# A two-block network on one core: the scheduler orders instructions on its timeline model

## The chip, the core and the metric

The kernel runs on one core of a Trainium2 chip, in one launch. The metric is the device time of that core in microseconds, the median of three runs. The engines are TensorE (PE: matmuls; PEld: its weight loads), VectorE (DVE), ScalarE (ACT), GpSimd (POOL) and SyncE (SP), which issues nearly all DMAs. Each engine works through its own list of instructions strictly in order, and semaphores make it wait for others.

## What is computed

The input is 256 tokens of width 1024, a context of 256 tokens, a condition vector and the weights of two blocks. The first block has four layers, the second has two:

```python
def first_block(x, p, ...):                     # DEPTH = 4
    for i in range(DEPTH):
        kind, j = i % N_MIXERS, i // N_MIXERS   # conv, ssm, rwkv, conv
        if kind == 0:
            y = short_conv_mixer(x, conv_w_in[j], conv_k[j], conv_w_out[j])
        elif kind == 1:
            y = s5_mixer(x, ...)
        else:
            y = rwkv7_mixer(x, ...)
        r = DN_ALPHA * x + y
        r = r + (p[i] @ ple_proj[i]) * jax.nn.sigmoid(r @ ple_gate[i])
        x = layer_norm(r, ln_g[i], ln_b[i])
    return x

def swiglu(h, w1, w3, w2):
    return (jax.nn.silu(h @ w1) * (h @ w3)) @ w2
```

Each layer of the second block is a half ffn (swiglu with 2816 hidden), a mixer and another half ffn, each behind an RMS norm that is shifted and scaled by values worked out from the condition (nine such vectors per layer and stream, called ada). Layer 0's mixer is attention of two kinds over tokens and context (mixer_ab), layer 1's is a chunked recurrence and a neighbourhood attention (mixer_cd). The context goes through ffns and the same attention of its own.

The parts that matter below are the rwkv mixer's end and the first conv:

```python
    mu_o = out.mean(-1, keepdims=True)
    var_o = jnp.square(out - mu_o).mean(-1, keepdims=True)
    out = ((out - mu_o) * lax.rsqrt(var_o + RWKV_GN_EPS)).reshape(bsz, seqlen, D_INNER)
    out = out * lnx_g.astype(f32) + lnx_b.astype(f32)
    ...
    return (out * jax.nn.silu(z)) @ w_out
```

## The kernel before

Activations lie transposed in SBUF, features on the 128 partitions in eight chunks, 256 tokens in the free direction. Every large product is done in three passes on values split in a high and a low part. `Net.get` (L590 to L607) brings in a weight tile of 128x1024 values: SP issues the DMA of 512 KB into `w` (L600), ScalarE copies the high part to `whi` (L601), VectorE subtracts it for the low part `wlo` (L602). `w` has four buffers, and `whi` and `wlo` four pairs. An output tile of 128x256 then takes 24 matmuls into a PSUM bank, eight chunks by three passes (`ps_mm`; three banks). Other banks are `ps_st` for sums over features, `ps_ca` and `ps_cb` for small products.

The program is written as Python generators, one for each chain of work (tokens, context, the heads of a mixer, preparation work on the side). `Net.weave` and `Net.par` pick which goes on, by a hand-made model of costs, and so lay down the program's order. Nothing of that is the engines' order yet. The kernel is recorded in a tile context (L1968), whose scheduler then goes through the program with the program's order as the priority: whenever an engine is free it takes the first instruction, in program order, that is ready by then. What "by then" means depends on a run of the program that the scheduler keeps beside it.

Three pieces of the program are spoken of later. In the first conv (`conv`, L720) the weights `in_conv_in` come as 32 tiles; while they stream, `ssm_prep` (L822) works on tables of the next layer on VectorE and ScalarE (tiles `ssm_s`, with DMAs `in_ssm_bc` at L891), and `load_context` (L1922) and `ada` (L1370) load `ctx` and `cond`. In `rwkv` (L1065), `heads` (L1178) runs for eight pairs of heads, up to three at a time on three sets of scratch (`rw_a0`, `rw_b0` to `rw_b2`). Each ends with four chunks of a state recurrence through `ps_cb` and `sv`, a norm over the head (`rsqrt`, L1336), and writes `r`. Behind the last of them the operand `mix` of the product for z takes the scratch slots of `rw_a1` and `rw_b1`, and `linear("rwkv_z", ...)` goes on with it. Beside all this the context's ffn runs (`ps_mm <- h1_hi, h1_lo`), which shares no data with the token stream. `rsqrt` (L679) is Ln, Exp and a square on ScalarE and two VectorE passes.

Where ScalarE's next function is not in the table that is loaded, an ACT_TABLE_LOAD stands before it; these are put in after the order is fixed.

## Time and profile before

| what | before |
|---|---|
| median of 3 runs | 2886.37 us (2886.14 to 2888.42) |
| profiled execution | 2890.76 us, of it 2889.0 us span from the first to the last instruction |
| TensorE busy | 2749.4 us (95% of the span) |
| VectorE busy | 2134.0 us (74%) |
| ScalarE busy | 1606.4 us (56%) |
| mean granted TensorE clock | 0.977 |
| DMA | 467.53 MB, engines busy 50% of the span |

The profiled execution is one execution of its own, with the profiler on; its time lies 4.4 us above the median of the others. An engine's busy share is a mean over very different stages.

### The profile page before, as it was taken

Reading aid. Unit: us, or ns where it says so; the run is one execution under the profiler, and the core shown is the slowest. Engines: PE = TensorE matmul, PEld = TensorE weight load, DVE = VectorE, ACT = ScalarE, POOL = GpSimd, SP = SyncE. Lnnn points to the kernel's source line nnn. Section 1 sums busy time; section 2 is a strip of 40 time slices with the busy share of each in tenths; the row PEclk is TensorE's granted clock in tenths of the full one; section 3 lists DMA queues with packets and bytes.
Section 4 is the critical chain, followed back from the end, with each engine's and each line's share of the span. In section 5 each row is a group of like instructions: output and inputs, shape, how many; then the busy total and the mean of one; then the engine's idle time right before and its main releaser. Section 6 shows DMA issues by size and latency. Waiting matters only on the chain.

```text
span 2889.0 us, 58552 instructions
## 1 busy us (share of the span) xinstructions
PE 2749.4 (95%) x23798; PEld 2604.6 (90%) x23798; DVE 2134.0 (74%) x3953; ACT 1606.4 (56%) x2976; POOL 14.8 (1%) x41
## 2 busy tenths in 40 slices
PE   8978799899999998999999999999999999999999
PEld 8967799778998998998999978999999999996999
DVE  8877777666688788899789887777855556676655
ACT  5455555766555465877666766445422234466443
POOL 0000000000000000000000000000000000000000
PEclk9989799999999999999999999999999999999999
DMA  7743355201586665666576644666543433222554
GB/s 270 238 165 110 108 167 175 82 17 40 163 269 226 220 197 167 209 215 203 182 226 195 199 130 155 203 225 194 180 142 125 139 117 103 89 82 65 161 182 139
DMA packets 132751, 467.53 MB, mean 162 GB/s; under 512 B 14720, under 2 KB 19072, under 8 KB 131840
## 3 DMA queue, kind: packets, MB, share of 16 engines
q1 hardware_dynamic: 132480, 463.78, 50.0%
q8 instruction: 187, 3.06, 0.4%
q14 instruction: 84, 0.69, 0.1%
HBM read 462.67 MB, written 1.05 MB: 161 GB/s over the span
## 4 chain that ended last, share of the span: by engine, by line
PE 72%; DVE 12%; DMA 7%; ACT 6%; issue 3%; SPq 0%; ACTq 0%; DVEq 0%
PE ps_mm L433 62%; PE ps_ca L433 5%; DMA w<-in_ada_dram 5%; DVE wlo L602 3%; PE ps_cb L433 2%; DVE junk L1379 2%; PE ps_st L433 2%; DVE ssm_m L403 2%; ACT whi L601 2%; DVE tc L403 1%; PE ps_cb L437 1%; ACT rw_b L403 1%; ACT L403 1%; ACT tc L403 1%; DMA w<-in_ab_in_dram 1%
## 5 line engine op out<-in xcount | busy, mean ns | idle before, releaser
L601 ACT ACTIVATE whi<-w 128x1024 fp32r<-128x1024 f32 (+1 forms) x687 | 715.9, 1043 | 740.2 <-PE ps_mm L433 488.1
L602 DVE TENSOR_TENSOR wlo<-w,whi 128x1024 fp32r<-128x1024 f32 (+1 forms) x687 | 825.6, 1203 | 239.2 <-ACT whi L601 236.8
L433 PE MATMUL ps_mm<-h_hi,whi 128*128 128x256 f32 x3024 | 873.1, 290 | 17.1 <-ACT h_hi L403 12.4
L433 PE MATMUL ps_mm<-h_hi,wlo 128*128 128x256 f32 x3024 | 859.5, 285 | 9.5 <-DVE wlo L602 9.5
L433 PE MATMUL ps_mm<-h_lo,whi 128*128 128x256 f32 x3024 | 856.5, 284 | 0.6 <-DVE h_lo L403 0.5
L433 PEld LDWEIGHTS ps_mm<-h_hi,whi 128*128 128x128 f32 x3024 | 573.6, 190 | 25.8 <-ACT h_hi L403 15.1
L433 PEld LDWEIGHTS ps_mm<-h_hi,wlo 128*128 128x128 f32 x3024 | 573.3, 190 | 12.2 <-DVE wlo L602 11.5
L433 PEld LDWEIGHTS ps_mm<-h_lo,whi 128*128 128x128 f32 x3024 | 577.5, 191 | 5.2 <-DVE h_lo L403 1.9
L1379 DVE SCALAR_TENSOR_TENSOR junk<-w,cond 128x1024 bf16<-128x1024 f32 x288 | 351.7, 1221 | 145.0 <-DMA w<-in_ada_dram 144.1
L433 PE MATMUL ps_mm<-d_hi,whi 128*128 128x256 f32 x1232 | 355.7, 289 | 4.1 <-DVE ctx L403 3.0
L433 PE MATMUL ps_mm<-d_hi,wlo 128*128 128x256 f32 x1232 | 350.4, 285 | 1.5 <-DVE wlo L602 1.5
L433 PE MATMUL ps_mm<-d_lo,whi 128*128 128x256 f32 x1232 | 349.2, 283 | 0.4 <-DVE d_lo L403 0.4
L433 PEld LDWEIGHTS ps_mm<-d_hi,whi 128*128 128x128 f32 x1232 | 232.3, 189 | 8.7 <-issue 5.7
L433 PEld LDWEIGHTS ps_mm<-d_lo,whi 128*128 128x128 f32 x1232 | 234.0, 190 | 3.4 <-issue 1.2
L433 PEld LDWEIGHTS ps_mm<-d_hi,wlo 128*128 128x128 f32 x1232 | 232.1, 189 | 2.8 <-DVE wlo L602 2.0
L403 DVE TENSOR_TENSOR td<-td,ps_mm 128x256 f32<-128x256 f32 x154 | 64.4, 418 | 70.0 <-PE ps_mm L433 68.9
L403 ACT ACTIVATE d_hi<-td 128x256 fp32r<-128x256 f32 x154 | 63.0, 409 | 89.5 <-DVE td L403 88.7
L403 ACT ACT_TABLE_LOAD x78 | 100.1, 1283 | 2.1 <-PEq L1964 0.7
L433 PE MATMUL ps_mm<-x_hi,whi 128*128 128x256 f32 x256 | 73.5, 287 | 12.0 <-ACT whi L601 12.0
L403 ACT ACTIVATE tc<-tc 128x256 f32<-128x256 f32 x182 | 75.1, 413 | 5.6 <-DVE tc L403 2.6
L433 PE MATMUL ps_mm<-xs_hi,whi 128*128 128x256 f32 x256 | 73.4, 288 | 4.8 <-ACT xs_hi L403 4.4
L403 ACT ACTIVATE td<-ps_mm 128x256 f32<-128x256 f32 x154 | 57.4, 374 | 32.9 <-PE ps_mm L433 32.3
(467 smaller groups left out, 5270.5 us busy)
## 6 DMA issues: line engine op xcount, KB each, us to landing
w<-in_ffn_in_dram SPq DMA_DIRECT2D x268, 512.0 KB, 4.2
w<-in_ada_dram SPq DMA_DIRECT2D x168, 512.0 KB, 4.3
w<-in_ffn_out_dram SPq DMA_DIRECT2D x96, 512.0 KB, 4.1
w<-in_conv_in_dram SPq DMA_DIRECT2D x64, 512.0 KB, 4.7
w<-in_ffn_out_dram SPq DMA_DIRECT2D x48, 384.0 KB, 3.1
w<-in_ab_in_dram SPq DMA_DIRECT2D x34, 512.0 KB, 4.4
w<-in_ple_gate_dram SPq DMA_DIRECT2D x32, 512.0 KB, 4.5
w<-in_conv_out_dram SPq DMA_DIRECT2D x16, 512.0 KB, 5.2
```

Of the source, the lines that this page charges most:

```text
L403: return f(**kw)
L433: self.t.matmul(out, lhsT=lhsT, rhs=rhs, start=start, stop=stop)
L437: self.t.transpose(out, in_, ident)
L601: nc.scalar.activation(out=hi[:, :n], in_=w[:, :n], func=AF.Copy)
L602: nc.vector.tensor_tensor(out=lo[:, :n], in0=w[:, :n], in1=hi[:, :n].bitcast(F32), op=ALU.subtract)
L1379: nc.vector.scalar_tensor_tensor(out=self.junk, in0=w, scalar=1.0, in1=cb[:, s], op0=ALU.mult, op1=ALU.mult, accum_out=m[:, t, s:s + 1])
```

## The change

One argument of the tile context: the scheduler keeps its timeline model beside it, instead of executing the program, to find out what is ready when.

```diff
@@ -1965,7 +1965,7 @@
-    with tile.TileContext(nc) as tc:
+    with tile.TileContext(nc, schedule_with_timeline_sim=True) as tc:
         program(tc, ap, out, pat, cat)
```

The instructions are the same, and so is their work (21145 matmuls, 920 DMAs issued by SP); only their order on each engine, and with it where they wait, is another. ScalarE's table loads go from 111 to 135. On TensorE 8640 matmuls stand at another place, nine in ten of the moves by fewer than 24 places, the largest by some 200 to 400; long stretches of ffn are untouched. Seen against the program's order, the new one takes more matmuls out of turn: 8700 stand elsewhere than in the program, where 2976 did before.

The first place is SP's queue at the start. Before, behind four weights of the first conv, with `ssm_s` the tables:

```order
L600 DMA w<-in_conv_in_dram 128x1024 x4
L891 DMA ssm_s_203<-in_ssm_bc_dram 128x1024 x2
L891 DMA ssm_s_201<-in_ssm_bc_dram 128x1024
L600 DMA w<-in_conv_in_dram 128x1024
L891 DMA ssm_s_201<-in_ssm_bc_dram 128x1024
L600 DMA w<-in_conv_in_dram 128x1024 x7
L1922 DMA ctx<-in_ctxT_dram 128x2048
```

The same place after; one weight stands ahead of these rows in both:

```order
L600 DMA w<-in_conv_in_dram 128x1024 x3
L891 DMA ssm_s_203<-in_ssm_bc_dram 128x1024 x2
L891 DMA ssm_s_201<-in_ssm_bc_dram 128x1024 x2
L1922 DMA ctx<-in_ctxT_dram 128x2048
L1370 DMA cond_157<-in_cond_dram 128x2048
L600 DMA w<-in_conv_in_dram 128x1024 x23
```

The fifth weight of the conv now stands behind all four tables, `ctx` and `cond`.

The second place is VectorE there. Before, from the fourth `wlo` (first row) to the fifth (last row); `tb <- ta, ps_mm` is a step of the conv:

```order
L602 TENSOR_TENSOR wlo<-w,whi 128x1024
L403 TENSOR_TENSOR ssm_s_159<-ssm_s_159 128x32
L403 TENSOR_TENSOR ssm_s_159<-ssm_s_159,pr 128x32
L403 TENSOR_TENSOR ssm_s_204<-ssm_s_203,ssm_s_159 128x512
L403 TENSOR_TENSOR ssm_s_159<-ssm_s_159 128x32 x2
L403 TENSOR_TENSOR tb<-ta,ps_mm 128x256
L403 TENSOR_TENSOR ssm_s_159<-ssm_s_159 128x32
L602 TENSOR_TENSOR wlo<-w,whi 128x1024
```

After, the last rows ahead of the fifth `wlo`; the fourth stands 33 rows before it:

```order
L403 TENSOR_TENSOR ssm_s_159<-ssm_s_159 128x32 x2
L403 TENSOR_TENSOR ta<-ta,te 128x256
L403 TENSOR_TENSOR ssm_s_159<-ssm_s_159 128x32
L403 TENSOR_TENSOR ta<-ta,ps_mm 128x256
L403 TENSOR_TENSOR ssm_s_159<-ssm_s_159 128x32 x4
L403 TENSOR_TENSOR ssm_s_202<-ssm_s_201,ssm_s_159 128x512 x2
L403 TENSOR_TENSOR ssm_s_159<-ssm_s_159 128x32
L403 TENSOR_TENSOR ssm_s_159<-ssm_s_201,ssm_s_159 128x512
L403 TENSOR_TENSOR ssm_s_202<-ssm_s_201,ssm_s_159 128x512
L602 TENSOR_TENSOR wlo<-w,whi 128x1024
```

Between the two low parts stand 16 operations on 128x512 tiles, 22 on 128x32 tiles and 5 steps of the conv, where there were one, five and one.

The third place is TensorE at the end of the rwkv heads. Before, around one of the last steps (`ps_cb_8898`) of the last head; the `ps_mm` rows are the context's ffn:

```order
L433 MATMUL ps_mm_8865<-h1_hi_3095,wlo_8861 128x256
L433 MATMUL ps_mm_8865<-h1_hi_3095,whi_8860 128x256
L433 MATMUL ps_mm_8865<-h1_lo_3096,whi_8860 128x256
L433 MATMUL ps_mm_8865<-h1_hi_3095,wlo_8861 128x256
L433 MATMUL ps_cb_8898<-rw_b1_5705,sv1_4505 64x64
L433 MATMUL ps_cb_8898<-rw_a1_5704 64x64
L433 MATMUL ps_cb_8898<-rw_b1_5705,sv1_4505 64x64
L433 MATMUL ps_cb_8898<-rw_a1_5704 64x64
L433 MATMUL ps_mm_8910<-h1_hi_3095,whi_8905 128x256
L433 MATMUL ps_mm_8910<-h1_lo_3096,whi_8905 128x256
L433 MATMUL ps_mm_8910<-h1_hi_3095,wlo_8906 128x256
L433 MATMUL ps_mm_8910<-h1_hi_3095,whi_8905 128x256
```

The same step after, up to the first matmul of the product for z (on `mix_hi`):

```order
L433 MATMUL ps_cb_8853<-sv1_4505,rw_b1_5705 64x64
L433 MATMUL ps_cb_8853<-rw_a1_5704 64x64
L433 MATMUL ps_cb_8853<-sv1_4505,rw_b1_5705 64x64
L433 MATMUL ps_cb_8853<-rw_a1_5704 64x64
L433 MATMUL ps_cb_8878<-rw_a1_5704,rw_b1_5705 64x64 x2
L433 MATMUL ps_cb_8898<-rw_b1_5705,sv1_4505 64x64
L433 MATMUL ps_cb_8898<-rw_a1_5704 64x64
L433 MATMUL ps_cb_8898<-rw_b1_5705,sv1_4505 64x64
L433 MATMUL ps_cb_8898<-rw_a1_5704 64x64
L433 MATMUL ps_st_8923<-rw_a1_5704,cs_base_155 128x256
L433 MATMUL ps_st_8941<-rw_b1_5705,cs_base_155 128x256
L433 MATMUL ps_mm_9158<-mix_hi_8971,whi_9153 128x256
```

The context's matmuls that stood between the steps, and four whole tiles of them that stood behind `ps_st_8941`, now stand ahead of the chain's last 30 matmuls.

## Rows read from the trace of the kernel before

**Rows 1.** The page's chain that ended last, share of the span by engine.

```profile
PE 72%; DVE 12%; DMA 7%; ACT 6%; issue 3%; SPq 0%; ACTq 0%; DVEq 0%
```

**Rows 2.** Windows: start and end, length, busy time by engine (instructions), clock, DMA share, GB/s.

```profile
0.00:2889.00 2889.00, 2749.42 (x23798) 2604.59 (x23798) 2133.98 (x3953) 1606.45 (x2976) 14.83 (x41) 0.98 0.50 162
178.00:330.00 152.00, 115.24 (x1150) 92.92 (x1151) 107.34 (x197) 80.36 (x181) 5.40 (x10) 0.80 0.29 91
755.00:784.00 29.00, 29.00 (x263) 27.45 (x262) 20.13 (x34) 18.16 (x37) 0.00 (x0) 1.00 0.64 200
1100.00:1700.00 600.00, 578.55 (x4387) 543.51 (x4386) 533.86 (x1039) 423.29 (x745) 0.00 (x0) 0.99 0.62 198
```

**Rows 3.** Timeline of SP's issues at the start: start us, us, engine, line, operation.

```profile
12.44 1.38 SPq L891 DMA_DIRECT2D ssm_s<-in_ssm_bc_dram  x3
```

**Rows 4.** DMA rate in 40 slices of 0 to 60 us.

```profile
GB/s 0 178 298 238 337 387 423 411 270 281 399 410 363 300 265 399 415 265 27 147 202 216 216 281 249 284 390 393 388 336 249 385 363 374 352 210 227 8 273 96
```

**Rows 5.** Timeline of VectorE at the start: start us, us, operation [idle before].

```profile
19.32 1.22 DVE L602 TENSOR_TENSOR wlo<-w,whi 128x1024 fp32r<-128x1024 f32 x1
20.45 0.19 DVE L403 TENSOR_TENSOR ssm_s<-ssm_s 128x32 f32<-128x32 f32 x1
...
20.66 0.69 DVE L403 TENSOR_TENSOR ssm_s<-ssm_s,ssm_s 128x512 f32<-128x512 f32 x1
...
21.90 1.23 DVE L602 TENSOR_TENSOR wlo<-w,whi 128x1024 fp32r<-128x1024 f32 x1
```

**Rows 6.** Timeline of TensorE at the start.

```profile
17.79 0.39 PE L433 MATMUL ps_mm<-x_hi,whi 128*128 128x256 f32 x1 [1.18 <-ACT whi L601]
...
26.53 0.28 PE L433 MATMUL ps_mm<-x_hi,wlo 128*128 128x256 f32 x1
```

**Rows 7.** Timeline of TensorE at the end of the rwkv heads.

```profile
764.17 0.34 PE L433 MATMUL ps_cb<-sv,rw_b 128*64 128x64 f32 x4
...
764.56 0.39 PE L433 MATMUL ps_mm<-h_hi,whi 128*128 128x256 f32 x1
...
771.88 0.60 PE L433 MATMUL ps_st<-rw_b,cs_base 128*128 128x256 f32 x2
...
783.83 0.29 PE L433 MATMUL ps_mm<-mix_hi,whi 128*128 128x256 f32 x1
```

**Rows 8.** Timeline of ScalarE there.

```profile
766.57 0.46 ACT L403 ACTIVATE sv<-ps_cb 64x64 f32<-64x64 f32 x2 [0.96 <-PE ps_cb L433]
...
773.31 1.28 ACT L394 ACT_TABLE_LOAD   x1
774.60 0.47 ACT L403 ACTIVATE tc<-ps_st,fixed 128x256 f32<-128x256 f32 x1
...
781.03 1.06 ACT L601 ACTIVATE whi<-w 128x1024 fp32r<-128x1024 f32 x1
782.05 1.03 ACT L403 ACTIVATE mix_hi<-ta 128x256 fp32r<-128x256 f32 x3
```

**Rows 9.** Timeline of VectorE there.

```profile
770.64 0.42 DVE L403 TENSOR_TENSOR rw_a<-rw_a,ps_st 128x256 f32<-128x256 f32 x1
...
781.48 0.48 DVE L403 SCALAR_TENSOR_TENSOR r<-rw_a,pr,r 128x256 f32<-128x256 f32 x1
```

**Rows 10.** Windows behind one wait of TensorE, columns as in rows 2.

```profile
884.70:892.00 7.30, 7.30 (x44) 7.19 (x45) 7.29 (x15) 4.67 (x14) 0.00 (x0) 0.70 0.37 100
892.00:900.00 8.00, 8.00 (x69) 8.00 (x68) 6.74 (x12) 5.22 (x7) 0.10 (x1) 1.00 0.83 267
```

**Rows 11.** Timeline of TensorE at four other waits.

```profile
119.58 0.38 PE L433 MATMUL ps_mm<-g_hi,whi 128*128 128x256 f32 x1 [2.16 <-ACT g_hi L403]
...
884.69 0.80 PE L433 MATMUL ps_mm<-xs_hi,whi 128*128 128x256 f32 x2 [4.45 <-ACT xs_hi L403]
...
2409.22 1.22 PE L433 MATMUL ps_st<-squares,cs_base 128*128 128x256 f32 x2 [3.15 <-DVE tc L403]
...
2629.67 0.65 PE L433 MATMUL ps_mm<-pt,vv 128*64 128x256 f32 x2 [1.37 <-ACT pt L403]
```

## The prediction

> **What bounds the kernel now.** The page's chain comes first: 72% of it is TensorE [rows 1]. The windows say the same: TensorE is busy 2749.4 us of 2889.0, at a granted clock of 0.98, VectorE 2134.0, ScalarE 1606.4 [rows 2]. So the change can only act on what TensorE doesn't do: 139.6 us of idleness, and some time at the lower clock. The instructions and their work stay what they are. A place where the new order makes TensorE wait costs that wait in full, since little slack follows (578.6 busy of 600 in 1100 to 1700 us [rows 2]), and a place where it now has something else to do gives back at most the wait that stood there. The working below is therefore a list of places, made by laying the two orders beside each other and reading the stretch concerned from the timeline of the engine that ends last there.
>
> **Place 1, the start.** The conv's weights come through one SP queue. Before, the fifth weight was issued ahead of the ssm tables, in a run of four that ends where the tables begin at 12.44 us [rows 3]. After, four tables (0.5 MB each) and then ctx and cond (1 MB each) stand ahead of it: 4 MB, at the 387 to 423 GB/s that a full queue shows [rows 4] some 10 us. On VectorE the fifth weight's low half started at 21.90, 2.6 us after the fourth's at 19.32 [rows 5]. In the new order 33 entries stand between the two: 16 operations on 128x512 tiles (0.69 us each, 0.60 from start to start [rows 5]), 22 on 128x32 (0.19 us, about 0.10 start to start, as the two from 20.45 to 20.66 show) and 5 steps of the conv (about 0.36 each from the kind of 0.42 us [rows 9]). That is 9.6 + 2.2 + 1.8 = 13.6 us. The fourth low half ends at about 20.5 as before (19.32 + 1.22), so the fifth ends at 20.5 + 13.6 + 1.2 = 35.3. TensorE's first matmul on it started at 26.53 [rows 6], so it is **8.8 us** late. A handful of matmuls that the new order puts ahead of it fill 0.5. The low bound is the queue's alone: counting the 10 us from 12.44, plus 1.3 for the weight's own 0.5 MB, 1.06 for its high half [rows 8] and 1.23 for the low one gives 26.0, no delay at all; counted from 18.2, the latest at which the fourth can have landed, it gives 31.8, 5 us. I take 8.8, because the engine's order is fixed and VectorE can't step past those entries. One gain stands here: the wait of 1.18 us at 17.79 [rows 6] gets 22 matmuls ahead of it and goes.
>
> **Place 2, the end of the rwkv heads.** The last head is a chain: matmuls into ps_cb, a copy by ScalarE, the next matmuls. Before, 12 matmuls of the context's ffn stood between any two steps; a step came every 2 us, and TensorE was busy 29.00 of 29.00 us from 755 to 784 [rows 2]. The head's norm (ps_st at 771.88) was followed by four whole context tiles, and the first matmul on mix began without a wait at 783.83 [rows 7]. In the new order those context matmuls have been spent earlier, where TensorE had hardly anything to fill. Nothing but the chain stands in the last 30 matmuls, then the ones on mix, whose operand lies in the slots of rw_a1 and rw_b1 and so can't be written before the norm is done: before, its high half started at 782.05, as soon as r was written at 781.48 plus 0.48 [rows 8, 9]. The price is the chain's own length. Seven rounds of 0.39 us matmuls (764.17 to 764.56 [rows 7]), a copy of 0.46 for two or half for one [rows 8] and 0.1 of handing over (estimate) are 7 x 0.84 = 5.9. Mean, subtraction, square and variance: two reductions of 0.60 (row 771.88 [rows 7]), two passes of 0.42 [rows 9], 0.3 of handing over, 2.3. Then Ln 0.47 [rows 8], eight passes of 0.4 to 0.48 on ScalarE and VectorE in turn down to the low half of mix [rows 8, 9], 0.8 of handing over and one table load of 1.28 [rows 8]: 6.0. In all 14.2, of which TensorE's own matmuls, which were there before too, are about 3.3 (7 x 0.39, and some 0.3 for each of the two reductions). So **11 us** of waiting. Bounds: without handing over and table load, with single copies only, 7; with two table loads and a weight's copy of 1.06 [rows 8] in front of every other step, 17.
>
> **The clock.** [...] Both places get it: +4.4.
>
> **What is given back.** Waits ahead of which the new order puts ready matmuls: thirteen, from 17.79 [rows 6] to 2629.67 [rows 11], together 16 us if each is filled to its length or by its number of matmuls at 0.12 us. At 119.58 fourteen matmuls come first, 1.7 of 2.16 us [rows 11]. In the norm behind the wait at 2409.22 [rows 11] and in one more like it three output tiles instead of two are taken up while the operands come in, 1.3 each by eleven more matmuls. For the others I take a quarter of the 13 us that are left, 3.3: most of them wait for a chain of VectorE and ScalarE, whose next link is put later by the same fill. Sum 7.6, and 1.1 at 17.79. If all were filled and the clock kept up at two of them it would be 16 + 2.6 + 4.4 = 23.
>
> **ScalarE's tables.** By the two orders loads go from 111 to 135, 24 x 1.28 us [rows 8] = 31 us on an engine that has 1282 us free [rows 2]. Twenty of the loads now stand between a norm's Ln and its Exp, most in the token and context attention. They delay chains that have fill, so I charge nothing for them, nor for chains of the attention heads that stand 20 to 120 matmuls later, except +2; without that cover it is the third rival. In the trace a load takes its 1.28 us and the next operation begins right behind it (773.31, then 774.60) [rows 8]. [...]
>
> **Sum.** 8.8 - 0.5 - 1.1 + 11 + 4.4 - 7.6 + 2 = **+17 us** on the profiled execution's 2890.8, so 2907 to 2908 in a profile. That execution is 4.4 above the median of the runs, and the forecast is for the median: 2886.4 + 17 = **2903 us**.
>
> **Rivals.**
> *Filled waits win (faster).* The engines' order is a guess about time, and TensorE has 139.6 us to win. If the fill pays in full (23), and places 1 and 2 come at their low bounds (0 and 7, with 2 of clock), the sum is -23 + 9 = -14: 2872 us. It decides where places 1 and 2 together cost less than what the fill returns. For it: the waits at 17.79 and 119.58 are plainly filled. Against: between 550 and 784 us and in the long matmul stretches there was next to nothing to fill. Chance 0.15.
> *No change.* The new order delays the chains but the stretches behind re-converge: where TensorE waits for VectorE's and ScalarE's own chains anyway (it is idle for 37 us from 178 to 330 us [rows 2]), arriving 9 us late at those costs nothing if these chains had run ahead meanwhile. Place 1 then drops out, and what is left is 11 + 2.2 + 2 - 7.6 = +8; with place 2 at its low bound, +4: 2890. Against it: the chains of that stretch start from matmul results. Chance 0.13.
> *The attention heads lose too (slower still).* If the twenty loads between Ln and Exp lie on chains that TensorE waits for, as place 2 does, each costs 1.28: +26 on the +17, 2929 us. Speaking for it: TensorE has only 21 us of idleness there now, so the cover is good and can only get worse. Against: no stretch there has its matmuls spent as at place 2; ready ffn tiles stand between the chains to the end. Chance 0.12.
>
> **How the numbers follow.** The forecast case (+6 to +34 us) has 0.60. Faster 0.15, same 0.13, slower 0.72, where 0.2% of the time, 5.8 us, is what a measurement here can tell from no change. The range reaches down to the filled waits, since their chance and the low bounds overlap, and up to the rival above: 2876 to 2930. Place 2 at its high bound (17) gives +23, 2909, inside it.
>
> **What would show it.** Place 1: a TensorE wait of 7 to 9 us near 27 us that ends with wlo, the fifth low half near 34 to 35, and a lower clock after it. Place 2: shortly before the first matmuls on mix, a run of waits for ScalarE copies of about 0.5 us each, then one of about 5 us, together 11, in a stretch that had none. Gains: no wait left near 18, at most half a microsecond where 119.58 stood. TensorE's busy time near 2749 us, with idleness up by some 13 us and the clock down to 0.97. The prediction is wrong if VectorE's entries at the start are waiting rather than working, if the copies between steps turn out to be covered by matmuls that I read as waiting for mix, or if TensorE's idleness goes up in the attention stretch (beyond 25 us from 1100 to 1700 us before shift).

## The result, and the profile after

The changed kernel takes **3037.83 us** (median of 4 runs, 3035.11 to 3038.47) against 2887.39 us for the one before on the same chip: ratio 1.0511, 95% interval 1.0496 to 1.0526. By the medians it is slower by 150 us (148 by the ratio, which is the measure used below) where I had forecast 17 and a range that ended at +44. The sign was right, the size was off by a factor of nine.

The page of the kernel after, its lines on the span, the busy time, the chain, and three groups:

```profile
span 3036.3 us, 58663 instructions
PE 2789.6 (92%) x23798; PEld 2630.2 (87%) x23798; DVE 2138.4 (70%) x3953; ACT 1637.5 (54%) x3000; POOL 14.6 (0%) x41
...
PE 47%; DVE 4%; ACT 4%; DMA 3%; issue 2%; DVEq 0%; ACTq 0%
...
L602 DVE TENSOR_TENSOR wlo<-w,whi 128x1024 fp32r<-128x1024 f32 (+1 forms) x687 | 825.0, 1203 | 268.6 <-ACT whi L601 264.5
...
L1379 DVE SCALAR_TENSOR_TENSOR junk<-w,cond 128x1024 bf16<-128x1024 f32 x288 | 351.6, 1221 | 183.8 <-DMA w<-in_ada_dram 182.5
...
L403 ACT ACT_TABLE_LOAD x102 | 130.9, 1283 | 2.5 <-PEq L1964 0.7
```

The same three groups on the page of the kernel before:

```profile
L602 DVE TENSOR_TENSOR wlo<-w,whi 128x1024 fp32r<-128x1024 f32 (+1 forms) x687 | 825.6, 1203 | 239.2 <-ACT whi L601 236.8
...
L1379 DVE SCALAR_TENSOR_TENSOR junk<-w,cond 128x1024 bf16<-128x1024 f32 x288 | 351.7, 1221 | 145.0 <-DMA w<-in_ada_dram 144.1
...
L403 ACT ACT_TABLE_LOAD x78 | 100.1, 1283 | 2.1 <-PEq L1964 0.7
```

The span grew by 147.3 us. TensorE idles for 3036.3 - 2789.6 = 246.7 us instead of 139.6 [rows 2], 107 more, and is busy 40 us longer with the same matmuls. Most of that is the clock: 166.9 us of its busy time lie at a granted clock of 0.50, 93.3 before, and there the matmuls of an output tile start 0.21 us apart instead of 0.12, so the 73.6 us more cost some 32 (an estimate from the two traces). VectorE and ScalarE do the work they did (24 more table loads apart), but VectorE now stands 39 us longer in front of `junk`, waiting for a DMA, and 29 us longer in front of `wlo`.

Windows of the kernel after (columns as in [rows 2]): the whole, the end of the rwkv heads, and the token and context attention, mixer_ab:

```profile
0.00:3036.30 3036.30, 2789.63 (x23798) 2630.20 (x23798) 2138.39 (x3953) 1637.48 (x3000) 14.60 (x41) 0.96 0.48 154
785.00:823.00 38.00, 25.86 (x197) 22.11 (x195) 22.47 (x46) 19.30 (x40) 0.00 (x0) 0.73 0.48 154
1150.00:1850.00 700.00, 625.04 (x4487) 571.95 (x4486) 558.78 (x1083) 460.26 (x787) 0.00 (x0) 0.95 0.54 173
```

The third stands for this window of the kernel before:

```profile
1100.00:1720.00 620.00, 598.55 (x4516) 558.75 (x4515) 549.55 (x1079) 435.57 (x770) 0.00 (x0) 0.99 0.61 195
```

About the same 4500 matmuls take 700 us instead of 620: 75.0 us of idleness instead of 21.5, and 26.5 us more of busy time at a clock of 0.95 instead of 0.99. More than half of the whole loss is here, where I had charged 2 us.

Where it is lost is seen best by counting TensorE's matmuls in order of time (the 21145 of the program). The table gives when the k-th starts in the trace of before, and how many microseconds later it starts in six others (the profiled executions; the experiments come below):

```
    k  before   after     e7     e8    e15    e17    e18
  500    74.8     8.2    8.9   -0.2    8.1    9.0    8.3   first conv
 1000   141.6     3.8    4.0    0.1    3.5    5.3    4.2
 3500   556.1    20.4   -1.6   -8.6   17.3   21.9   16.7
 5000   722.6    18.0   -2.0   -8.8   16.3   19.5   14.2
 5500   784.8    34.1   13.0   -8.8   31.3   35.8   30.0   end of the rwkv heads
 6000   846.8    37.2   13.8   -7.6   33.9   42.3   33.1
 6500   917.9    48.2   26.4   -7.4   45.3   54.0   44.8   norm behind rwkv
 8000  1106.4    51.4   24.8   -8.2   46.8   57.2   48.3   mixer_ab begins
 8500  1186.3    52.7   23.8   -9.6   45.8   58.3   47.6
 9000  1256.2    71.3   33.5  -10.3   45.8   76.2   65.5
11000  1528.5    82.9   38.4  -11.0   44.5   87.5   77.1
12000  1667.4   124.3   70.9  -11.1   44.8  105.6  119.8   end of the heads of mixer_ab
13000  1829.9   132.9   76.1  -10.8   46.5  113.5  129.2
15000  2075.4   141.3   84.2   -9.7   54.6  122.8  138.0
20500  2805.7   147.8   85.8  -10.9   59.3  126.2  141.5
```

In the long ffn stretches (13000 to 14500, 15000 to 17500) the delay doesn't change at all: the loss has places.

**Three places.** At the start (timelines of TensorE, VectorE and ScalarE after, columns as in [rows 5, 6]), the fifth weight:

```profile
31.45 0.58 PE L433 MATMUL ps_mm<-x_hi,whi 128*128 128x256 f32 x1 [6.29 <-ACT whi L601]
...
32.59 1.22 DVE L602 TENSOR_TENSOR wlo<-w,whi 128x1024 fp32r<-128x1024 f32 x1
...
27.61 1.89 ACT L403 ACTIVATE cond<-cond 128x2048 f32<-128x2048 f32 x1
29.41 1.04 ACT L403 ACTIVATE ssm_s<-ssm_s 128x1024 f32<-128x1024 f32 x1
30.36 1.04 ACT L601 ACTIVATE whi<-w 128x1024 fp32r<-128x1024 f32 x1
```

TensorE waits 6.29 us, and what ends it is the high half, not the low one: ScalarE's list has `cond` and a table in front of it. VectorE's low half starts at 32.59 where it started at 21.90 [rows 5].

At the end of the rwkv heads, TensorE and ScalarE after:

```profile
800.52 0.27 PE L433 MATMUL ps_cb<-rw_a 128*64 128x64 f32 x1 [1.59 <-DVE rw_a L403]
...
805.01 0.47 PE L433 MATMUL ps_cb<-sv,rw_b 128*64 128x64 f32 x2 [1.82 <-DVE rw_a L403]
...
810.59 1.22 PE L433 MATMUL ps_st<-rw_b,cs_base 128*128 128x256 f32 x2 [0.96 <-ACT rw_b L403]
817.03 1.01 PE L433 MATMUL ps_mm<-mix_hi,whi 128*128 128x256 f32 x3 [5.21 <-ACT mix_hi L403]
...
810.56 1.28 ACT L403 ACT_TABLE_LOAD   x1
811.85 0.47 ACT L403 ACTIVATE tc<-ps_st,fixed 128x256 f32<-128x256 f32 x1
812.34 1.28 ACT L403 ACT_TABLE_LOAD   x1
813.64 0.86 ACT L403 ACTIVATE tc<-tc 128x256 f32<-128x256 f32 x2
```

From 799 to 818 there are nine waits, together 11.3 us, the last of 5.21; and the Ln stands between two loads, one for itself and one for the Exp behind it. The two stretches of the granted clock there, in windows:

```profile
785.00:801.50 16.50, 13.67 (x129) 12.30 (x127) 13.75 (x24) 10.38 (x19) 0.00 (x0) 1.00 0.85 279
801.50:822.00 20.50, 11.19 (x63) 8.81 (x62) 8.72 (x22) 8.93 (x21) 0.00 (x0) 0.50 0.20 60
```

And at the end of mixer_ab's heads, TensorE, ScalarE and VectorE after:

```profile
1773.84 0.82 PE L433 MATMUL ps_ca<-tb,second 128*128 128x256 f32 x2 [2.13 <-DVE tb L403]
1782.21 1.22 PE L433 MATMUL ps_ca<-tb,second 128*128 128x256 f32 x2 [7.55 <-DVE tb L403]
...
1773.41 1.28 ACT L403 ACT_TABLE_LOAD   x1
1774.71 0.47 ACT L403 ACTIVATE tc<-ps_mm,fixed 128x256 f32<-128x256 f32 x1
1775.20 1.28 ACT L403 ACT_TABLE_LOAD   x1
1776.49 0.86 ACT L403 ACTIVATE tc<-tc 128x256 f32<-128x256 f32 x2
...
1777.39 0.42 DVE L403 SCALAR_TENSOR_TENSOR tc<-ps_mm,tc 128x256 f32<-128x256 f32 x1 [0.19 <-ACT tc L403]
...
1778.70 1.23 DVE L1379 SCALAR_TENSOR_TENSOR junk<-w,cond 128x1024 bf16<-128x1024 f32 x1 [0.23 <-DMA w<-in_ada_dram]
...
1780.53 1.22 DVE L1379 SCALAR_TENSOR_TENSOR junk<-w,cond 128x1024 bf16<-128x1024 f32 x1
...
1781.67 0.48 DVE L403 SCALAR_TENSOR_TENSOR tb<-qb,pr,tc 128x256 f32<-128x256 f32 x1
```

The reader is to see what place 2 was, a second time and longer. The last head's norm has no matmul left to hide behind (TensorE's last ready ones end at 1771.7), so its chain is paid in full: two loads, and two `junk` sums of 1.2 us that VectorE has in its list ahead of the chain's next step. Before, the same norm ran between ffn matmuls, and TensorE was busy 77.7 of 80 us from 1600 to 1680.

### The profile page after: what moved, and what is told of

Its sections match the earlier page's. It is cut to its first block, busy times and chain, and to the rows that moved or that the text cites. A ratio compares the mean times of both kernels' runs of the same rounds, so it can differ in the third digit from the quotient of the medians.

```text
span 3036.3 us, 58663 instructions
## 1 busy us (share of the span) xinstructions
PE 2789.6 (92%) x23798; PEld 2630.2 (87%) x23798; DVE 2138.4 (70%) x3953; ACT 1637.5 (54%) x3000; POOL 14.6 (0%) x41
## 4 chain that ended last, share of the span: by engine, by line
PE 47%; DVE 4%; ACT 4%; DMA 3%; issue 2%; DVEq 0%; ACTq 0%
PE ps_mm L433 43%; PE ps_ca L433 2%; DMA w<-in_ada_dram 2%; ACT L403 1%; DVE wlo L602 1%; DVE junk L1379 1%; ACT whi L601 1%; PE ps_cb L433 1%; PE ps_cb L437 1%; DVE tc L403 1%; PE ps_st L433 1%; ACT tc L403 0%; DMA w<-in_ffn_in_dram 0%; ACT L394 0%; ACT p L403 0%
## 5 line engine op out<-in xcount | busy, mean ns | idle before, releaser
L433 PE MATMUL ps_mm<-h_lo,whi 128*128 128x256 f32 x3024 | 867.8, 288 | 11.1 <-DVE h_lo L403 11.0
L433 PEld LDWEIGHTS ps_mm<-h_hi,wlo 128*128 128x128 f32 x3024 | 581.1, 192 | 6.3 <-DVE wlo L602 2.4
L1379 DVE SCALAR_TENSOR_TENSOR junk<-w,cond 128x1024 bf16<-128x1024 f32 x288 | 351.6, 1221 | 183.8 <-DMA w<-in_ada_dram 182.5
L403 ACT ACT_TABLE_LOAD x102 | 130.9, 1283 | 2.5 <-PEq L1964 0.7
L403 ACT ACTIVATE h_hi<-tc,mod 128x256 fp32r<-128x256 f32 x88 | 41.1, 502 | 63.6 <-DVE tc L403 63.4
```

The lines of the kernel that those rows point to most:

```text
L403: return f(**kw)
L433: self.t.matmul(out, lhsT=lhsT, rhs=rhs, start=start, stop=stop)
L1379: nc.vector.scalar_tensor_tensor(out=self.junk, in0=w, scalar=1.0, in1=cb[:, s], op0=ALU.mult, op1=ALU.mult, accum_out=m[:, t, s:s + 1])
```

## The experiments

In all of them the instructions are those of the kernel (exceptions are named), and the order of chosen engines is held by edges that carry order alone. `scheduled` builds the program once more, only to read the order that the other scheduler gives:

```diff
+def pin(tc, order, spans):
+    nosync = mybir.DependencyInfo(mybir.DependencyClass.NoSync, mybir.DependencyReason.DATA)
+    here = {i.name: i for i in tc.nc.cur_bb.bb.instructions}
+    for engine, lo, hi in spans:
+        names = [n for n in order["EngineType." + engine] if n in here and lo <= int(n.split("-")[1]) < hi]
+        for a, b in zip(names, names[1:]):
+            tc.add_manual_dep(here[b], a, nosync, reason="pin")
...
+    order = scheduled(arrays, pat, cat, False)
     with tile.TileContext(nc, schedule_with_timeline_sim=True) as tc:
         program(tc, ap, out, pat, cat)
+        pin(tc, order, [("PE", 0, 1000000000)])
```

The last argument of `scheduled` says whose order (False: the scheduler of before), `spans` which engine and which instructions by their number in the program; the rest is ordered by the timeline model around them. "Loss" below is (ratio - 1) x 2889 us; the ratios' intervals are plus or minus 0.0010 to 0.0025, 3 to 7 us. The kernel after has a loss of 148.

### One engine's order, or two

e1 is the diff above. The others differ in the last line (e2 swaps the two schedulers):

```diff
-        pin(tc, order, [("PE", 0, 1000000000)])
+        pin(tc, order, [("DVE", 0, 1000000000), ("Activation", 0, 1000000000)])   # e3
+        pin(tc, order, [("PE", 0, 1000000000), ("DVE", 0, 1000000000)])           # e5
+        pin(tc, order, [("PE", 0, 1000000000), ("Activation", 0, 1000000000)])    # e6
```

e1, TensorE as before. 

> The changed kernel, but TensorE's matmuls are held in the order that they had before (edges of order alone, no waits); the other engines are still ordered on the timeline model. Theory A (the loss lies in TensorE's order: ready matmuls are taken too early, and then a chain stands alone): the time of before comes back, 2887 us within 12. Theory B (the loss lies in VectorE's and ScalarE's orders, chain steps behind weight splits and sums): little comes back, 3000 us or more. Theory C (the 24 more table loads, which fall to 114 here with before's 111): about 2890 too, so this run parts A from B only.

e2, the scheduler of before, TensorE as after. 

> The kernel before, but TensorE's matmuls held in the changed kernel's order; the rest ordered as before, around that. Theory A: the loss is here in full, 3037 us within 25. Theory B: 2887 to 2920. Theory C (127 table loads, 16 of the 24 more): two thirds of the loss, about 2987.

e3, VectorE and ScalarE as before. 

> The changed kernel, but VectorE and ScalarE held in the order of before (111 table loads as before); TensorE and the queue ordered on the timeline model. Theory A: TensorE's order is still that model's, so at least 100 of the 150 us remain: 2985 or more, unless the held engines draw TensorE's order with them. Theories B and C: 2890 within 12.

e5, TensorE and VectorE as before. 

> As e1 (timeline model, TensorE in the order of before), with VectorE held in the order of before as well; ScalarE and the queue are left to the model (116 table loads). After e1, where 3096 us came out with TensorE's order of before, the loss must lie in one of the other two engines. Theory V (VectorE's order: chain steps behind weight splits and condition sums): 2890 to 2910. Theory S (ScalarE's order): 3050 or more.

e6, TensorE and ScalarE as before. 

> The counterpart: TensorE and ScalarE held in the order of before (111 table loads), VectorE and the queue left to the model. Theory V: 3050 or more, as e1. Theory S: 2890 to 2910.

| kernel | held in the order of before | us | ratio, 95% interval | loss |
|---|---|---|---|---|
| e1 | TensorE | 3095.51 | 1.0711 (1.0687 to 1.0735) | 205 |
| e3 | VectorE, ScalarE | 2998.68 | 1.0374 (1.0351 to 1.0398) | 108 |
| e5 | TensorE, VectorE | 2953.23 | 1.0220 (1.0198 to 1.0242) | 64 |
| e6 | TensorE, ScalarE | 3071.26 | 1.0621 (1.0601 to 1.0640) | 179 |
| e2 | TensorE as after, the rest ordered around it by before's scheduler | 3025.03 | 1.0466 (1.0446 to 1.0486) | 135 |

That TensorE's order is the cause falls with e1: the old order alone makes it worse. And with the old lists on two engines, the one that the timeline model still orders around them (e3: TensorE, e5: ScalarE, e6: VectorE) costs 108, 64 and 179 us, 351 in all where the three together cost 148. e5, at 2953 us, meets neither of its theories. And e2 came out where theory A had it, 3037 within 25: with the rest ordered around it by the scheduler of before, TensorE's new order brings 135 of the 148 us; but to put the old one back, as in e1, doesn't take them away. A list is good or bad only with the lists it was made with.

### All three engines, or one place

e16 holds all three; e15 holds them only in mixer_ab, e17 only in its last part, and e18 there TensorE alone:

```diff
+        pin(tc, order, [("PE", 0, 1000000000), ("DVE", 0, 1000000000), ("Activation", 0, 1000000000)])  # e16
+        pin(tc, order, [("PE", 12949, 21500), ("DVE", 12949, 21500), ("Activation", 12949, 21500)])  # e15
+        pin(tc, order, [("PE", 18700, 20120), ("DVE", 18700, 20120), ("Activation", 18700, 20120)])  # e17
+        pin(tc, order, [("PE", 18700, 20120)])  # e18
```

e16. 

> The timeline model, with TensorE, VectorE and ScalarE held in the order of before over the whole program; only SP's queue is its own. Theory E (the orders of the three engines together are the whole loss, no single one of them): 2887 to 2895, the low bound of place 1 (queue alone, 0 to 5 us) included. Rival S (the order of SP's DMAs is a cost of its own): 2900 or more, with waits on DMA under wlo, whi and junk.

e15. 

> The kernel after, with TensorE, VectorE and ScalarE all held in the order of before for the instructions of mixer_ab alone, the rest free to the timeline model; SP stays free. Theory P (the loss has places: the attention of tokens and context costs what the comparison of the two traces shows there, 77 us): 2955 to 2970. Rival N (what is lost is lost where two orders meet, as the mixed orders of one or two engines showed): above 3000, with new waits at the edges of the stretch.

e17. 

> The kernel after, with TensorE, VectorE and ScalarE held in the order of before for the last part of mixer_ab alone (the last norms of the attention heads beside the second matmul of the context's ffn, some 95 us of before), where the two traces part by 35 us. Theory P (the loss has places, also at this size): 35 us of the 150 come back, 2998 to 3008. Rival N (the new order in front of the part has already spent the matmuls and put off the chains, so that the old order only waits for them elsewhere): under 15 us, 3023 or more.

e18. 

> The same part, but with TensorE alone in the order of before. Theory F (what costs there is that TensorE spends the context's matmuls ahead of the last chains, as my place 2 has it): most of what the run with three engines gives comes back. Rival C (the chains' steps are put off on VectorE and ScalarE as well, and TensorE in the old order waits for them one after another): no gain, or up to 40 us slower, 3035 to 3075.

| kernel | us | ratio, 95% interval | loss | given back |
|---|---|---|---|---|
| e16 | 2896.58 | 1.0017 (1.0006 to 1.0028) | 5 | 143 |
| e15 | 2953.87 | 1.0218 (1.0205 to 1.0232) | 63 | 85 |
| e17 | 3004.49 | 1.0389 (1.0375 to 1.0404) | 112 | 35 |
| e18 | 3034.80 | 1.0493 (1.0478 to 1.0507) | 142 | 5 |

e16: the orders of TensorE, VectorE and ScalarE together are the loss. (2896.58 us lies between the ranges of theory E and rival S; by the ratio it is 2894, in E's.) What is left, 2 to 8 us, stands at the start: the 500th matmul is 6.2 us late, with SP's queue alone in the new order. ScalarE waits there for the fifth weight:

```profile
26.77 1.06 ACT L601 ACTIVATE whi<-w 128x1024 fp32r<-128x1024 f32 x1 [5.61 <-DMA w<-in_conv_in_dram]
```

e15: theory P holds at its full size, 85 us where the traces showed 80 for the stretch, and the table's column is flat from 8500 to 13000. e17: theory P again, 35 us. (Its profiled execution was the slowest of five, 12 us above their median and later from the rwkv part on; the table's step from 11000 to 12000 falls from 41.4 to 18.1 us in it.) e18: with TensorE alone, nothing comes back that is clear of the intervals. TensorE's waits from 1690 to 1800 us, after, in e18 (to 1810) and in e17, the longest rows of each (us in total, times, longest):

```profile
PE ps_ca L433 <- DVE tb L403: 10.2, 3, 7.5
PE ps_mm L433 <- ACT ta L403: 5.0, 1, 5.0
PE ps_mm L433 <- ACT td L403: 4.8, 3, 2.7
```

```profile
PE ps_ca L433 <- DVE tb L403: 16.6, 7, 4.1
```

```profile
PE ps_ca L433 <- ACT p L403: 3.7, 1, 3.7
PE ps_ca L433 <- DVE tb L403: 2.3, 4, 0.6
```

With its old order TensorE still has the ffn matmuls to put between the steps, but now it stands in line for steps that VectorE takes late: seven waits of 16.6 us in place of three of 10.2. Rival C holds: the fill that was spent early and the chain that was put off are one thing, on three engines.

### The start and the rwkv heads

e4 holds SP and VectorE in the first conv, e11 TensorE in the rwkv heads:

```diff
+        pin(tc, order, [("SP", 0, 1300), ("DVE", 0, 1300)])   # e4
+        pin(tc, order, [("PE", 5700, 9240)])                  # e11
```

e4. 

> The changed kernel, but SP's queue and VectorE held in the order of before for the first conv alone. Place 1 of the prediction (the fifth weight behind tables and condition) gives back 8 to 10 us: 3028 us. If that delay is taken up later by chains that TensorE waits for anyway, it gives back nothing: 3037 within 2.

e11. 

> The changed kernel, with TensorE alone held in the order of before, and only from the rwkv heads to the product for z (about 3460 of its matmuls). Place 2 of the prediction, with 19 us measured where 13 were forecast: 13 to 19 us come back, 3018 to 3024. If VectorE's order holds the chain up there too, less than 8: above 3029.

e4 took 3031.70 us, 1.0478 (1.0453 to 1.0502), a loss of 138. The delay at the 500th matmul falls from 8.2 to 0.1 us, so place 1 is made by the orders of SP and VectorE there; at the 20000th 4 us of this are left (144.1 against 147.8). By the ratios it is 10 us, but their intervals overlap.

e11 took 3044.80 us, 1.0542 (1.0526 to 1.0559), a loss of 157: no gain. The step from the 5000th to the 5500th matmul falls from 16.2 to 6.4 us, and the stretch in front of it, 3500 to 5000, goes from -2.5 to +11.0. What holds for e18 holds here: the old order of one engine waits elsewhere.

### ScalarE's table loads

e7 and e8 hold all orders of after and of before, and make the functions that need tables Identity times 0 on tiles of more than 8 columns (those with a running sum excepted), which leaves 34 loads. e13 and e14 keep all work: on ScalarE each Exp of a norm stands right behind its Ln, and the load of the table with both stands where the Ln finds another.

```diff
+            if PLAIN[0] and kw.get("func") in ONE_SET and "accum_out" not in kw and free_size(outs[0]) > 8:
+                kw.update(func=AF.Identity, scale=0.0)          # e7, e8
...
+    act = [n for n in order["EngineType.Activation"] if n not in LOADS]
+    act = [m for n in act if n not in pull for m in ((n, pair[n]) if n in pair else (n,))]
+    for n in act:                                               # e13, e14
+        f = func[n]
+        if f == AF.Ln and state != "ln":
+            need.add(LNS.index(n))
+            state = "ln"
```

e7. 

> The changed kernel with every engine held in its own order, and ScalarE's table functions replaced by Identity with scale 0 (same sizes; softmax's Exp with its sum and two 128x8 Exps stay), so that the 102 table loads that are put in after the ordering are gone, up to one; the 33 that stand in the program remain. The output is not the reference's. Theory L (the loads, which no ordering saw, make ScalarE late and the order wrong): within 30 us of e8, near 2870. Theory G (the order itself takes long work ahead of chains, loads or not): 100 us or more above e8.

e8. 

> The same replacement in the kernel before, every engine held in the order of before: 78 loads less. Both theories: a little faster than 2887, 2850 to 2885, since few of its chains wait for ScalarE; it is the measure for e7.

e13. 

> The kernel after with all its orders held, but on ScalarE each norm's Exp directly behind its Ln, and the load of the table that holds both directly ahead of those Ln that find another table: 98 loads instead of 135. It computes everything. Theory T (the loads that the new order puts between Ln and Exp lie on the chains that TensorE waits for, and they are what the removal of nearly all loads gave back): most of the 58 us that went with 101 loads goes here with 37, so 2985 to 3005. Rival W (a load costs the same wherever it stands, 58 / 101 = 0.57 us each): 37 x 0.57 = 21, so 3016. Rival O (the waits are there anyway, the loads only fill them): 3030 to 3038.

e14. 

> The same rule on the kernel before: 104 loads instead of 111. Theory T: 7 loads on chains at 1.3 us, most of what all loads cost there (2887 to 2880), so 2880 to 2884. Rival W: 7 x 10 / 77, under 1 us, 2886 to 2888. Moving Exp ahead of other work could also delay that work: up to 2892.

| kernel | loads | us | ratio, 95% interval | loss | a load taken away |
|---|---|---|---|---|---|
| e7 (after) | 135 to 34 | 2980.10 | 1.0312 (1.0291 to 1.0332) | 90 | 58 / 101 = 0.57 us |
| e8 (before) | 111 to 34 | 2879.91 | 0.9960 (0.9944 to 0.9975) | -12 | 12 / 77 = 0.15 us |
| e13 (after) | 135 to 98 | 3015.09 | 1.0429 (1.0416 to 1.0442) | 124 | 24 / 37 = 0.64 us |
| e14 (before) | 111 to 104 | 2890.74 | 1.0005 (0.9996 to 1.0015) | 1 | none seen |

Without tables the two orders are still 102 us apart (90 + 12), so the loads carry some 46 of the 148. In mixer_ab, from the 8500th to the 13000th matmul, e7 falls 53.5 us further behind e8 (33.4 to 86.9 in the table) where the kernel after falls 80.2 behind the one before: some 27 of its 80 us there are tables. e13 says that those between Ln and Exp aren't dearer than others: rival W, 0.57 us each and 3016 us, met the 3015.09. It has fewer loads than the kernel before, 98 against 111, and is still 124 us behind it. The page of e13, its two groups of loads:

```profile
L403 ACT ACT_TABLE_LOAD x64 | 82.1, 1283 | 1.8 <-PEq L2028 0.7
L526 ACT ACT_TABLE_LOAD x34 | 43.6, 1283 | 0.6
```

### VectorE's steps ahead of its background work

In the attention stretch VectorE's chain steps start 1.2 us after their last operand was written, before 0.8 us (an estimate from the two traces: means over some 660 steps, operands by their tiles' names without buffer numbers, lags of over 50 us left out), often behind a `junk` or `wlo`. e9 and e10 move these in VectorE's list behind steps that were ready by the trace (after: 401 behind 587; before: 292 behind 411), all else held; e12 is e9 with e7's replacement.

```diff
+    for e, moved in MOVED.items():
+        new = ["I-" + n for n in moved]
+        at, mine = set(new), iter(new)
+        order["EngineType." + e] = [next(mine) if n in at else n for n in order["EngineType." + e]]
```

e9. 

> The changed kernel with all engines held in its own order, except that on VectorE 401 weight splits and condition sums (1.2 us each) are put behind 587 short steps of chains, always such as had their operands in the changed kernel's trace when the long operation began, and at most 1.6 us of them. Softmax steps and a stretch around 1900 us are left alone. Theory G (the order puts long background work ahead of chain steps that are ready): 50 us or more come back, 2985 or less. If VectorE's part lies elsewhere (its waits for TensorE or for ScalarE's loads): less than 20, above 3017.

e10. 

> The same rule applied to the kernel before, from its own trace: 292 splits and sums behind 411 ready steps, everything else held. Theory G says that there is little of it here, as TensorE waits 140 us in all: 0 to 15 us faster, 2875 to 2888. If splits that come later make TensorE wait for weights: slower.

e12. 

> e9 with e7's replacement (table functions as Identity with scale 0, so that the 102 loads are gone; the output is not the reference's). If loads and VectorE's order are two causes that add up: e7's 2980 less what e9 gained, 2920 or so with a gain of 60. If they are one cause (loads make the order wrong): no faster than 2970.

| kernel | us | ratio, 95% interval | loss | against |
|---|---|---|---|---|
| e9 | 3063.72 | 1.0608 (1.0591 to 1.0624) | 176 | after: 28 more |
| e10 | 2924.11 | 1.0129 (1.0108 to 1.0150) | 37 | before: 37 more |
| e12 | 3006.99 | 1.0413 (1.0393 to 1.0434) | 119 | e7: 29 more |

The gain that the theory promised doesn't come, and the repair costs 28 to 37 us wherever it is made. TensorE's waits, after and in e9, in the row that grew most:

```profile
PE ps_mm L433 <- DVE wlo L602: 3.7, 4, 1.3
```

```profile
PE ps_mm L433 <- DVE wlo L602: 14.8, 12, 3.5
```

A `wlo` that steps back makes the ffn's matmuls late, and these are the fill. That is 11 of the 28 us; from before to e10 the same row grows only from 11.5 to 15.1 us, so where most of the 37 go isn't shown. `junk`'s wait for its DMA did fall, from 183.8 to 110.1 us, and bought nothing.

## Why the prediction was wrong

**What held.** The method of places, with TensorE's idleness and clock as what can change: 107 us of the 147 in the traces are idleness, and of the 40 of longer busy time most are clock. Place 1: 8.8 us forecast, 8.3 at the 250th matmul and 8.2 at the 500th, 8.1 of it gone in e4. The engine I named was half right: VectorE's low half came about as late as I had it (32.59 against some 34; the 33 entries that I counted are rows, and hold the 43 operations that I summed), but the wait ended with ScalarE's high half. And the queue alone, which I had at 0 to 5 us, makes 6.2 of the 8.2 (e16). Place 2: 11 us forecast, 11.3 measured, with a run of short waits and a last one of 5.21 as described, though the two longest of the short ones (1.59 and 1.82) end with VectorE's `rw_a` and not with a copy by ScalarE. The fills: the waits at 17.79 [rows 6] and 119.58 [rows 11] are gone, and the delay falls by 4.4 us from the 500th to the 1000th matmul and by 6.4 from the 3500th to the 4000th. I had 7.6 us for all fills but the first, and 1.1 for that one; how much of the two falls is theirs wasn't tried by itself.

**The clock, mis-sized.** The sum has 4.4 us for it, 2.2 at each of the two places (an estimate that can be worked out from [rows 10]); no run shows this term. In its place they showed this. At place 1 the granted clock after is 0.50 from 30.07 to 36.90, with TensorE busy for 4.85 us of these, so some 2.1 us (an estimate at starts 0.21 us apart instead of 0.12). At place 2 the granted clock fell from 1.00 to 0.50 at 801.5, in a run of short waits and ahead of the long one, and stayed there for 20.5 us: the matmuls on `mix` start 0.21 us apart until 821.9, and 0.12 from 822.05 on. From the 5250th to the 5500th matmul 18.8 us were lost, 11.3 by waiting, so 7.5 otherwise. In all it is some 32 us, of 40 us of longer busy time, in place of 4.4.

**The step that failed** is this one: "They delay chains that have fill, so I charge nothing for them, nor for chains of the attention heads that stand 20 to 120 matmuls later, except +2". The sign that I had named for its failure came: idleness in the stretch rose by 54 us, where I allowed 25. The stretch lost 80 us by the traces, and e15 gave back 85. I had read the cover off the trace of before, where the fill stands between the steps, and took it for a property of the stretch. It was a property of the order: the new one spends the context's matmuls earlier, here as at place 2, and the chains' last steps then stand alone; and these steps come later on VectorE as well, so that TensorE's old order alone found them late (e18). Of my rivals the third had the place, but priced it by 20 loads of 1.28 us each; the loads are the smaller part, and its 2929 us would have been 109 too low. Also missed were the norm behind rwkv (11 us from the 6000th to the 6500th matmul), 8 us between 2010 and 2075 (the table's step from 13000 to 15000), and the norm behind the first conv: from the 1200th to the 1400th matmul, 168 to 222 us before, the delay goes from 4.0 to 17.4 us. TensorE waits there 7.9, 7.1 and 4.6 us for `total`, `x` and `y`, where it waited 3.9, 3.4 and 1.3. The first two I had not looked up in the order, and in the third stretch the rival of no change had the delay of place 1 taken up, where it grew; no run tried any of the three by itself. At the norm behind rwkv, VectorE and TensorE after:

```profile
918.00 1.23 DVE L602 TENSOR_TENSOR wlo<-w,whi 128x1024 fp32r<-128x1024 f32 x1 [1.11 <-ACT whi L601]
...
919.81 1.22 DVE L1379 SCALAR_TENSOR_TENSOR junk<-w,cond 128x1024 bf16<-128x1024 f32 x1
...
927.11 1.23 DVE L1379 SCALAR_TENSOR_TENSOR junk<-w,cond 128x1024 bf16<-128x1024 f32 x1 [3.66 <-DMA w<-in_ada_dram]
...
923.51 2.93 PE L433 MATMUL ps_st<-sq,cs_base 128*128 128x256 f32 x6 [10.16 <-DVE sq L403]
931.36 1.01 PE L433 MATMUL ps_mm<-xs_hi,whi 128*128 128x256 f32 x3 [4.92 <-ACT xs_hi L403]
```

The sums of squares wait 10.16 us in one piece, because most additions on VectorE have a `wlo` or `junk` in front of them; then a `junk` that waits 3.66 us for its DMA stands ahead of the norm's next step, which starts at 928.66 where ScalarE had its operand ready at 927.84. Before, the two waits were 1.24 and 4.45 us (the second in [rows 11]).

**Table loads.** Charged at nothing for the covered ones; by e7 and e8 they carry 46 us of the difference. 24 more loads don't make this at 0.6 us each (14): the loads as a whole cost more in the new order, 0.57 us against 0.15 for each one taken away; that there is less to hide them is the reading that fits, not one that was tried by itself. On ScalarE itself a load takes 1.28 us after too (1283 ns in the mean of each page), and the next operation begins right behind it: at 1773.41 the load, at 1774.71 the Ln.

**Shown and not shown.** Shown: the loss is in the orders of the three compute engines together (e16), has places (e15, e17), couldn't be had back at two of them through TensorE alone (e11, e18), and is by some 46 us a matter of tables (e7, e8). What remains open is what the timeline model takes for shorter or earlier than it is on the chip, so that it spends the fill: no run separates its beliefs on DMAs, on waits between engines and on table loads. For the 63 us outside mixer_ab the places stand in the table, but only the start was tried by itself with success; the rest wasn't held with three engines. No version that does all the work beat the kernel before: e14 and e16 come within 1 and 5 us of it.

## What to carry to other kernels

Cover is a property of an order, not of a stretch: before charging a delayed chain at nothing because matmuls stand beside it, look up in the new order whether these still stand there when its last links come, in every stretch that has such chains and not only at the first two. The engines' lists are fitted to each other, so an order is changed on all of them or not at all; here one list of the other scheduler among the old ones cost 64 to 179 us, and moving background work behind ready steps on one engine cost 28 to 37. To find where a reordering loses, compare when the k-th matmul starts in both traces, and hold all engines of one stretch to the old order.

## What the runs showed of the hardware

That the clock would be over a fifth of the loss (some 32 of 148 us, an estimate from the two traces) was not expected: the same 23798 matmul records are 2789.6 us busy at a mean granted clock of 0.959 and 2749.4 at 0.977 [rows 2]. It wasn't the long waits alone: at place 2 the granted clock went from 1.00 to 0.50 at 801.5, behind waits of 0.87, 1.59 and 0.37 us, and came back to 1.00 at 822.0, 5 us after the last wait, with matmuls on `mix` in between. And a table load, 1.28 us on ScalarE in both orders, had no one price in the kernel's time: each one taken away gave back 0.15 us in the order of before (e8) and 0.57 to 0.64 in the order of after (e7, e13).
